# Low-rank first products of the time mixing: four float32 products against twelve products of rounded and low parts

## The chip, the cores and the metric

The kernel runs on one core of one Trainium2 chip. Its engines are TensorE (PE, with its weight loads shown apart as PEld), VectorE (DVE), ScalarE (ACT), GpSimd (POOL) and SyncE (SP), which here only issues DMA transfers. The metric is device time in microseconds (us) of one execution; less is better. A product of 128 x 128 weights with 128 x N operands is one matmul that reads both operands from SBUF and adds into PSUM.

## The reference, cut to what matters

The program is a two-layer trunk over 256 tokens of 2048 channels. Layer 0 is an RWKV-7 time mixing and a squared-ReLU MLP; layer 1 is a band attention and an MLP. The change lies in the first stage of layer 0 alone:

```python
h = modulate(rms_norm(x, g_mix[0]), sh1, sc1)
xx = token_shift(h) - h
xr, xw, xk, xv, xa, xg = [h + xx * mu[j] for j in range(6)]
v = xv @ w_v                                   # 2048 x 2048
w_log = -softplus(-(w0 + tanh(xw @ w1) @ w2)) - 0.5   # w1: 2048 x 96
a = sigmoid(a0 + (xa @ a1) @ a2)                      # a1: 2048 x 96
g = sigmoid(xg @ g1) @ g2                             # g1: 2048 x 256
```

The products concerned are `xw @ w1`, `xa @ a1` and `xg @ g1`, the "low-rank first products". All of it is float32, and the output is compared with float32 results.

## The kernel before

Activations lie with channels on the 128 partitions and the 256 tokens along the free axis, so each tensor of 2048 channels is 16 tiles of 128 x 256 (KT = 16). Large products are not computed in float32 directly. Each operand is split in two parts of type float32r: the rounded part H (a ScalarE cast, L384 for weights, L577 for activations) and the low part L, operand minus H (a VectorE subtraction, L387 for weights, L578 for activations). Three products are then summed in PSUM: H by H, H by L and L by H. The low-rank first products are the exception: they are float32 matmuls on the unsplit operands (L803, L807).

The first stage, `layer_a` up to L825, runs one loop over the 16 channel tiles n:

- SyncE loads `lw` (L787: 448 columns, the rows n of w1, a1 and g1 side by side) and the first 1024 columns of row n of w_v (`raw`, L374).
- Steps of a generator, `ada_blocks`, compute shift and scale (the adaLN of c) that later tiles need. Each step uses one 512 KB tile `rawa`: one half of them goes through TensorE (L696), the other through a VectorE multiply with accumulation (L702). A block of steps serves two tiles n (the last two blocks serve one each), eight `rawa` tiles to a block of two. At its end come L707, L712, L717 to L721.
- VectorE and ScalarE make h of tile n (L794, L796), GpSimd the difference xx (`diff`, L740), VectorE the mixed inputs (`mixed`, L745), in the order 3 (for v), 1, 4, 5 (low-rank), 2 (for k), each in one of four `mix` buffers. L820 makes the sixth in place.
- The mixed input 3 is split. Then come the four float32 products into the two accumulators `pl` (L803: w1 and a1, 96 columns each; L807: two halves of g1), and 24 matmuls of eight output tiles for the first half of v (L811 to L813).
- From n = 4 on, `v_part` adds 24 more matmuls (L773 to L775) for the second half of v, whose weights come in pieces (`v_part_weight`); n = 14 and 15 run two of them, and two more follow the loop.

After the loop the sums in `pl` go through tanh, copy and sigmoid (L830 to L832) with changes of ScalarE's function table; then the pairs of heads follow, whose projections for k and r (L418, L419) keep TensorE full for the rest of layer 0.

The order on each engine's queue is not simply the program's. The framework plans the program with its own estimate of each instruction's duration, and lets an instruction of lower rank go ahead where its operands are ready earlier in that plan; the engines then work through their queues in that fixed order. SyncE's queue is one of them, so a load that waits for its buffer holds all later loads. Buffers rotate: `raw` has six, `rawa` six, `lw` three, the weights' H and L three each.

Of the kernel before, what the change touches and what calls it, by code (L numbers as in the profile page):

```python
# [12 lines left out]
F32 = mybir.dt.float32  # L13
F32R = mybir.dt.float32r
AF = mybir.ActivationFunctionType
ALU = mybir.AluOpType
AX = mybir.AxisListType

P = 128
D = 2048  # L20
T = 256
# [9 lines left out]
HK = 8  # L31
# [304 lines left out]
class Body:  # L336
# [303 lines left out]
    def layer_a(self, st, sp):  # L640
        nc, tc, d = self.nc, self.tc, self.d
# [5 lines left out]
        with ExitStack() as s1:  # L647
# [3 lines left out]
            ph = s2.enter_context(tc.tile_pool(name="ph", bufs=1))  # L651
            s3 = s2.enter_context(ExitStack())
            pb = self.np = s3.enter_context(tc.tile_pool(name="pb", bufs=1))
            h = ph.tile([P, KT, T + 1], F32, name="h")
            first = CST_AT["ui"][0]
            nc.scalar.dma_start(out=self.csts[:, :first], in_=d["cst"][:, :first])
            for q in range(4):
# [7 lines left out]
            nc.vector.memset(h[:, :, 0:1], 0.0)  # L665
            gain = self.gp.tile([P, KT], F32, name="gain_g_mix0")
            sums = pb.tile([P, 2, KT], F32, name="sums01")
            rawa = lambda: pb.tile([P, HK * P], F32, tag="rawa", bufs=6, name="rawa")

            crow, diag = self.wp.tile([P, HK * P], F32, tag="acc", bufs=1, name="crow"), rawa()  # L670
            nc.vector.tensor_tensor(out=diag.rearrange("p (k n) -> p k n", n=P),
                                    in0=self.cst("ident").unsqueeze(1).to_broadcast([P, HK, P]),
                                    in1=self.ct[:, HK:].unsqueeze(2).to_broadcast([P, HK, P]), op=ALU.mult)
            for i in range(0, HK * P, 512):
                ps = pp.tile([P, 512], F32, tag="t", bufs=1, name="t")
# [51 lines left out]
            adab = ada_blocks()  # L727
            ss = pp.tile([P, 2, T], F32, tag="v3", bufs=1, name="v3")[:, 0, :]
            for n in range(KT):
                sq = pb.tile([P, T], F32, tag="sq", bufs=3, name="sq")  # L730
                nc.scalar.activation(sq, h[:, n, 1:T + 1], AF.Square)
                nc.tensor.matmul(ss, self.cst("ones"), sq, start=(n == 0), stop=(n == KT - 1))
            r = self.rstd(ss)
# [4 lines left out]
            def diff(n):  # L738
                xx = ph.tile([P, T], F32, tag="xx", bufs=2, name="xx")
                nc.gpsimd.tensor_tensor(out=xx, in0=h[:, n, 0:T], in1=h[:, n, 1:T + 1], op=ALU.subtract)  # L740
                return xx

            def mixed(m, n, xx):
                t = ph.tile([P, T], F32, tag="mix", bufs=4, name="mix")
                nc.vector.scalar_tensor_tensor(out=t, in0=xx, scalar=self.vec(f"mu{m}", n),  # L745
                                               in1=h[:, n, 1:T + 1], op0=ALU.mult, op1=ALU.add)
                return t
# [3 lines left out]
            pl = [pp.tile([P, 2, T], F32, tag=f"l{i}", bufs=1, name=f"l{i}") for i in range(2)]  # L751
# [6 lines left out]
            def v_part_weight():  # L758
                src = next(coming, None)
                return None if src is None else self.halves(self.raw(src))  # L760

            def v_part():

                lo, nk, i = next(parts)
                H, L = self.v_next
                nt = 8 // nk
                sums = [pp.tile([P, 2, T], F32, tag=t, bufs=1, name="t") for t in "tm"[:nt // 2]]
                for k in range(nt):
                    for kt in range(nk):
                        j, ps = nt * kt + k, sums[k // 2][:, k % 2, :]  # L770
                        a, b = (xv[:, lo + kt, i_, 0:T] for i_ in range(2))
                        last = k % 2 == 1 and kt == nk - 1
                        nc.tensor.matmul(ps, H[:, j, :], a, start=(k % 2 == 0 and kt == 0), stop=False)  # L773
                        nc.tensor.matmul(ps, H[:, j, :], b, start=False, stop=False)
                        nc.tensor.matmul(ps, L[:, j, :], a, start=False, stop=last)  # L775
                self.v_next = v_part_weight()
                for k, ps in enumerate(sums):
                    o = 8 + nt * i + 2 * k
                    o = v[:, o:o + 2, :]
                    if lo == 0:  # L780
                        nc.scalar.copy(o, ps)
                    else:
                        nc.vector.tensor_tensor(out=o, in0=o, in1=ps, op=ALU.add)

            for n in range(KT):
                lw = pb.tile([P, 448], F32, tag="lw1", bufs=3, name="lw1")
                nc.sync.dma_start(out=lw, in_=d["lora1"][n // 4, :, n % 4, :])  # L787
                raw = self.raw(d["w_v_rows"][n])
                ahead = 5 if n + 2 < KT and ends[n + 1] == n + 2 else 0
                while adab_at < min(4 * KT, 4 * ends[min(n + 1, KT - 1)] + ahead):  # L790
                    next(adab)
                    adab_at += 1
                hn = h[:, n, 1:T + 1]
                nc.vector.scalar_tensor_tensor(out=hn, in0=hn, scalar=gain[:, n:n + 1], in1=r,  # L794
                                               op0=ALU.mult, op1=ALU.mult)
                nc.scalar.activation(hn, hn, AF.Identity, bias=self.mods[(0, 0)][:, n:n + 1])  # L796
                xx = diff(n)
                first, last = n == 0, n == KT - 1
                self.split(xv, n, mixed(3, n, xx))
                H, L = self.halves(raw)  # L800

                for i, m in enumerate((1, 4)):
                    nc.tensor.matmul(pl[0][:96, i, :], lw[:, i * 96:(i + 1) * 96], mixed(m, n, xx),  # L803
                                     start=first and i == 0, stop=last and i == 1)
                t = mixed(5, n, xx)
                for i in range(2):
                    nc.tensor.matmul(pl[1][:, i, :], lw[:, 192 + i * P:192 + (i + 1) * P], t,  # L807
                                     start=first and i == 0, stop=last and i == 1)
                for i in range(8):
                    ps = pv[i // 2][:, i % 2, :]  # L810
                    nc.tensor.matmul(ps, H[:, i, :], xv[:, n, 0, 0:T], start=first and i % 2 == 0, stop=False)  # L811
                    nc.tensor.matmul(ps, H[:, i, :], xv[:, n, 1, 0:T], start=False, stop=False)
                    nc.tensor.matmul(ps, L[:, i, :], xv[:, n, 0, 0:T], start=False, stop=last and i % 2 == 1)  # L813
                if n == 3:
                    self.v_next = v_part_weight()
                for _ in range((n >= 4) + (n >= KT - 2)):
                    v_part()
                self.split(xk, n, mixed(2, n, xx))

                nc.vector.scalar_tensor_tensor(out=hn, in0=xx, scalar=self.vec("mu0", n), in1=hn,  # L820
                                               op0=ALU.mult, op1=ALU.add)
# [17 lines left out]
        with ExitStack() as s1:  # L839
# [57 lines left out]
            for slot in range(S * NPAIR + Pair.STEPS):  # L897
# [9 lines left out]
                last = self.last_pe()  # L907
                for _, _, pr in sorted(live, key=lambda x: x[:2]):
                    with tc.issue_after(last):
                        next(pr.gen)  # L910
                    last = self.last_pe()
# [329 lines left out]
```

## Time and profile before

| | us |
|---|---|
| median of 3 runs | 2670.8 |
| lowest and highest | 2667.13, 2671.81 |
| the profiled execution | 2666.43 |
| its span, first to last instruction | 2664.6 |
| the first stage, from the start to the last low-rank product | about 184 |

The stage of the change is about 7% of the span; beyond it nothing is edited. Times in the views are us from the start of the span. A group's row gives a line, an engine, an operation, the tile written and the tiles read, the shape, the count, the busy time and the mean duration in ns, and the idle time of that engine just before with what ended it. [...]

### The profile page before, as it was taken

Reading aid. Unit: us, or ns where it says so; the run is one execution under the profiler, and the core shown is the slowest. Engines: PE = TensorE matmul, PEld = TensorE weight load, DVE = VectorE, ACT = ScalarE, POOL = GpSimd, SP = SyncE. Lnnn points to the kernel's source line nnn. Section 1 sums busy time; section 2 is a strip of 40 time slices with the busy share of each in tenths; the row PEclk is TensorE's granted clock in tenths of the full one; section 3 lists DMA queues with packets and bytes.
Section 4 is the critical chain, followed back from the end, with each engine's and each line's share of the span. In section 5 each row is a group of like instructions: output and inputs, shape, how many; then the busy total and the mean of one; then the engine's idle time right before and its main releaser. Section 6 shows DMA issues by size and latency. Waiting matters only on the chain.

```text
span 2664.6 us, 58295 instructions
## 1 busy us (share of the span) xinstructions
PE 2584.6 (97%) x23596; PEld 2225.7 (84%) x23596; DVE 2107.8 (79%) x3102; ACT 1368.2 (51%) x2516; POOL 217.8 (8%) x336
## 2 busy tenths in 40 slices
PE   7998999999999999999999999999999999999997
PEld 4787778777899888888888998877898888888886
DVE  6888988888889888888888898899887556555555
ACT  3345656556455355355365554565564464453554
POOL 0001323222100000000001100000100000000002
PEclk9999999999999999999999999999999999999998
DMA  9976656566778899889998779888766555555553
GB/s 348 319 244 193 205 188 200 180 207 192 260 235 307 310 325 326 322 322 333 323 327 290 232 245 329 314 272 264 263 218 233 187 187 189 190 189 186 187 189 119
DMA packets 207149, 662.62 MB, mean 249 GB/s; under 512 B 21408, under 2 KB 54560, under 8 KB 206880
## 3 DMA queue, kind: packets, MB, share of 16 engines
q1 hardware_dynamic: 204816, 656.36, 72.9%
q8 instruction: 185, 3.03, 0.5%
q10 hardware_dynamic: 2064, 2.54, 0.3%
q14 instruction: 84, 0.69, 0.1%
HBM read 656.72 MB, written 2.10 MB: 247 GB/s over the span
## 4 chain that ended last, share of the span: by engine, by line
PE 85%; DVE 5%; issue 4%; ACT 3%; DMA 3%; POOL 1%; SPq 0%; DVEq 0%; ACTq 0%; POOLq 0%
PE pj L418 45%; PE pj L419 22%; PE pj L408 2%; PE pj L407 2%; PE pj L409 2%; DVE wL L387 2%; DMA raw<-w_ada 1%; PE iv L111 1%; ACT wH L384 1%; DVE acc L460 1%; PE gr L105 1%; PE o L407 1%; PE ms L330 1%; DMA raw<-w_q 1%; PE m L696 0%
## 5 line engine op out<-in xcount | busy, mean ns | idle before, releaser
L387 DVE TENSOR_TENSOR wL<-raw,wH 128x1024 fp32r<-128x1024 f32 x772 | 942.0, 1221 | 351.9 <-ACT wH L384 347.1
L384 ACT CAST wH<-raw 128x1024 fp32r<-128x1024 f32 x772 | 805.8, 1045 | 784.3 <-PE pj L418 625.5
L418 PE MATMUL pj<-aHL,wH 128*128 128x512 f32 x3328 | 1196.4, 401 | 1.1 <-DVE x L954 1.1
L419 PE MATMUL pj<-aHL,wL 128*128 128x256 f32 x3328 | 937.2, 282 | 0.4 <-DVE wL L387 0.3
L418 PEld LDWEIGHTS pj<-aHL,wH 128*128 128x128 f32 x3328 | 630.0, 189 | 151.7 <-issue 8.1
L418 PE MATMUL pj<-hHL,wH 128*128 128x512 f32 x2048 | 722.4, 398 | 0.0
L419 PEld LDWEIGHTS pj<-aHL,wL 128*128 128x128 f32 x3328 | 630.0, 189 | 2.5 <-issue 0.8
L419 PE MATMUL pj<-hHL,wL 128*128 128x256 f32 x2048 | 573.7, 280 | 0.9 <-DVE wL L387 0.9
L418 PEld LDWEIGHTS pj<-hHL,wH 128*128 128x128 f32 x2048 | 384.6, 188 | 94.5 <-DVE hHL L1000 0.2
L419 PEld LDWEIGHTS pj<-hHL,wL 128*128 128x128 f32 x2048 | 386.5, 189 | 1.3 <-DVE wL L387 1.2
L460 DVE SCALAR_TENSOR_TENSOR acc<-rada,ct,acc 128x1024 f32<-128x1024 f32 x256 | 327.6, 1280 | 9.6 <-DMA rada<-w_ada 9.1
L524 POOL TENSOR_TENSOR ss<-ss,sq 128x256 f32<-128x256 f32 x56 | 54.6, 975 | 1588.5 <-ACT sq L523 1588.2
L1025 DVE SCALAR_TENSOR_TENSOR x<-pj,mod,x 128x256 f32<-128x256 f32 x256 | 123.4, 482 | 58.3 <-PE pj L419 54.6
L460 DVE SCALAR_TENSOR_TENSOR acc<-raw,ct,acc 128x1024 f32<-128x1024 f32 x104 | 137.6, 1323 | 10.7 <-DMA raw<-w_ada 10.3
L997 ACT ACTIVATE t<-t 128x256 f32<-128x256 f32 x112 | 46.8, 418 | 123.7 <-DVE t L969 123.7
L407 PE MATMUL pj<-aHL,wH 128*128 128x258 f32 x384 | 109.0, 284 | 0.0
L408 PE MATMUL pj<-aHL,wH 128*128 128x258 f32 x384 | 108.9, 284 | 0.0
L409 PE MATMUL pj<-aHL,wL 128*128 128x258 f32 x384 | 108.0, 281 | 0.0
L409 PEld LDWEIGHTS pj<-aHL,wL 128*128 128x128 f32 x384 | 73.2, 191 | 0.2
L408 PEld LDWEIGHTS pj<-aHL,wH 128*128 128x128 f32 x384 | 72.6, 189 | 0.1
L407 PEld LDWEIGHTS pj<-aHL,wH 128*128 128x128 f32 x384 | 72.2, 188 | 0.2
L999 ACT ACTIVATE t<-t 128x256 f32<-128x256 f32 x128 | 53.4, 417 | 3.4
(252 smaller groups left out, 2842.8 us busy)
## 6 DMA issues: line engine op xcount, KB each, us to landing
raw<-w_up SPq DMA_DIRECT2D x256, 512.0 KB, 4.5
raw<-w_down SPq DMA_DIRECT2D x256, 512.0 KB, 4.5
rada<-w_ada SPq DMA_DIRECT2D x209, 512.0 KB, 5.6
raw<-w_ada SPq DMA_DIRECT2D x111, 512.0 KB, 4.5
rada<-w_ada_kv SPq DMA_DIRECT2D x64, 512.0 KB, 6.5
rawa<-w_ada SPq DMA_DIRECT2D x32, 512.0 KB, 6.9
rawa<-w_ada_t SPq DMA_DIRECT2D x32, 512.0 KB, 7.1
raw<-w_k SPq DMA_DIRECT2D x32, 512.0 KB, 4.2
```

The source lines that it names most:

```text
L384: nc.scalar.copy(Hf, raw)
L387: eng.tensor_tensor(out=Lf, in0=raw, in1=Hf, op=ALU.subtract)
L407: nc.tensor.matmul(ps, H[:, i, :], a(kt)[:, 0, :], start=(first and kt == 0), stop=False)
L408: nc.tensor.matmul(ps, H[:, i, :], a(kt)[:, 1, :], start=False, stop=False)
L409: ins = nc.tensor.matmul(ps, L[:, i, :], a(kt)[:, 0, :], start=False, stop=(last and kt == KT - 1))
L418: nc.tensor.matmul(ps, H[:, i, :], a(kt), start=(kt == 0), stop=False)
L419: ins = nc.tensor.matmul(ps[:, 0, :], L[:, i, :], a(kt)[:, 0, :], start=False, stop=(kt == KT - 1))
L460: nc.vector.scalar_tensor_tensor(out=self.acc, in0=raw, scalar=ck, in1=self.acc, op0=ALU.mult, op1=ALU.add)
L524: (eng or nc.gpsimd).tensor_tensor(out=self.ss, in0=self.ss, in1=sq, op=ALU.add)
L997: nc.scalar.activation(t, t, AF.Relu)
L999: nc.scalar.activation(t, t, AF.Square)
L1025: nc.vector.scalar_tensor_tensor(out=x, in0=ps[:, i, :], scalar=self.mods[(layer, 5)][:, n:n + 1], in1=x, op0=ALU.mult, op1=ALU.add)
```

## The change

The three mixed inputs 1, 4, 5 and the tile `lw` are split as the large products' operands are: ScalarE casts the rounded parts (one cast of 448 columns, three of 256), and GpSimd, not VectorE, subtracts to make the low parts. Each of the four float32 products becomes three float32r products, H by H, H by L and L by H. These twelve matmuls are placed after the v matmuls and the `v_part` of the same n, where the four were ahead of them. A new tile `lwh` has one buffer, `mh` has three. To make room, `rawa` goes from six buffers to five, `sq` (used ahead of the loop) from three to two, and `lw` from three to two.

```diff
-            rawa = lambda: pb.tile([P, HK * P], F32, tag="rawa", bufs=6, name="rawa")
+            rawa = lambda: pb.tile([P, HK * P], F32, tag="rawa", bufs=5, name="rawa")
...
-                sq = pb.tile([P, T], F32, tag="sq", bufs=3, name="sq")
+                sq = pb.tile([P, T], F32, tag="sq", bufs=2, name="sq")
...
-                lw = pb.tile([P, 448], F32, tag="lw1", bufs=3, name="lw1")
+                lw = pb.tile([P, 448], F32, tag="lw1", bufs=2, name="lw1")
...
-                for i, m in enumerate((1, 4)):
-                    nc.tensor.matmul(pl[0][:96, i, :], lw[:, i * 96:(i + 1) * 96], mixed(m, n, xx),
-                                     start=first and i == 0, stop=last and i == 1)
-                t = mixed(5, n, xx)
-                for i in range(2):
-                    nc.tensor.matmul(pl[1][:, i, :], lw[:, 192 + i * P:192 + (i + 1) * P], t,
-                                     start=first and i == 0, stop=last and i == 1)
+                lwh = pb.tile([P, 2, 448], F32R, tag="lwh", bufs=1, name="lwh")
+                nc.scalar.copy(lwh[:, 0, :], lw)
+                mhs = []
+                for m in (1, 4, 5):
+                    t = mixed(m, n, xx)
+                    mh = ph.tile([P, 2, T], F32R, tag="mh", bufs=3, name="mh")
+                    nc.scalar.copy(mh[:, 0, :], t)
+                    nc.gpsimd.tensor_tensor(out=mh[:, 1, :], in0=t, in1=mh[:, 0, :], op=ALU.subtract)
+                    mhs.append(mh)
+                nc.gpsimd.tensor_tensor(out=lwh[:, 1, :], in0=lw, in1=lwh[:, 0, :], op=ALU.subtract)
                 for i in range(8):
...
                 for _ in range((n >= 4) + (n >= KT - 2)):
                     v_part()
+                for i in range(4):
+                    mh, lo = mhs[min(i, 2)], (0, 96, 192, 192 + P)[i]
+                    w = 96 if i < 2 else P
+                    ps = pl[i // 2][:w, i % 2, :]
+                    for a, b, s_ in ((0, 0, first and i % 2 == 0), (0, 1, False), (1, 0, False)):
+                        nc.tensor.matmul(ps, lwh[:, a, lo:lo + w], mh[:, b, :], start=s_,
+                                         stop=last and i % 2 == 1 and a == 1)
                 self.split(xk, n, mixed(2, n, xx))
```

## The prediction, made before the changed kernel ran

> **What bounds the kernel now.** I read the page's first part, the busy times stretch by stretch, and then the chain of waits through the first stage.
>
> ```profile
> PE 2584.6 (97%) x23596; PEld 2225.7 (84%) x23596; DVE 2107.8 (79%) x3102; ACT 1368.2 (51%) x2516; POOL 217.8 (8%) x336
> ```
>
> Over the whole span TensorE is full, but the edit touches about 156 us only, so that share decides nothing. The next rows are busy time, with instructions in brackets, for PE, PEld, DVE, ACT and POOL, then TensorE's granted clock, the DMA share and GB/s.
>
> ```profile
> 30.00:60.00 30.00, 26.57 (x199) 20.22 (x200) 26.22 (x55) 7.57 (x14) 2.97 (x3) 0.84 1.04 375
> 90.00:120.00 30.00, 27.61 (x241) 22.24 (x241) 25.05 (x52) 10.65 (x18) 1.18 (x2) 1.00 0.89 300
> 150.00:180.00 30.00, 28.11 (x269) 24.59 (x270) 27.82 (x58) 11.36 (x20) 3.62 (x3) 1.00 0.76 260
> ...
> 30.00:186.00 156.00, 140.57 (x1260) 113.66 (x1261) 132.02 (x260) 54.96 (x89) 13.01 (x15) 0.97 0.91 313
> ```
>
> From 30 to 186 us VectorE is busy for 132.02 of 156 us (85%), TensorE for 140.57, the DMA engines for 91%; ScalarE has 101 us free and GpSimd 143. Three resources are nearly full, and the chain tells which ends last:
>
> ```profile
> 110.13 1.10 PE l L803 x4
> ...
> 118.79 0.14 PE t L775
> ...
> 119.97 1.15 DVE wL L387
> ...
> 121.16 0.38 PE t L775
> ...
> 128.11 0.13 PE t L775
> ...
> 128.87 1.23 DVE wL L387
> ...
> 130.14 0.39 PE t L775
> ...
> 131.25 0.86 PE l L803 x4
> 132.11 0.57 PE m L696 x8
> ...
> 133.71 0.86 PE l L807 x4
> ...
> 136.18 0.12 PE v L812
> ...
> 137.38 0.12 PE t L773
> ...
> 203.03 0.29 PE pj L418
> ```
>
> Between the first rows matmul follows matmul. TensorE stops at 118.93 until 121.16 and at 128.24 until 130.14, about 4 us in a block of 21.1 us (from L803 at 110.13 to L803 at 131.25), and both times what comes last is a weight's low part on VectorE. So the stage's time is TensorE's work plus VectorE's lateness; a microsecond off TensorE's queue counts if VectorE keeps up, and a microsecond onto VectorE's dense stretches counts nearly whole.
>
> **The change part by part.**
>
> *TensorE.* Four L803 records take 0.86 us, and so do four of L807. Each float32 product makes two records, as these counts for 32 products per line show:
>
> ```profile
> L803 PE MATMUL l<-mix,lw 128*96 128x256 f32 x64 | 17.9, 401 | 5.2 <-DVE mix L745 5.2
> L807 PE MATMUL l<-mix,lw 128*128 128x256 f32 x64 | 18.2, 410 | 0.0
> ...
> L577 ACT CAST aHL<-mix 128x256 fp32r<-128x256 f32 x32 | 13.0, 406 | 58.5 <-DVE mix L745 58.5
> ...
> L384 ACT CAST wH<-raw 128x1024 fp32r<-128x1024 f32 x29 | 30.0, 1043 | 3.6 <-issue 2.5 <-PE v L812 0.8 <-PE t L774 0.3
> ...
> L745 DVE SCALAR_TENSOR_TENSOR mix<-xx,vecs,h 128x256 f32<-128x256 f32 x80 | 36.3, 498 | 6.0 <-POOL xx L740 5.9
> ```
>
> One float32 product is therefore 0.43 us. Ten float32r starts lie between 136.18 and 137.38, so one costs 0.12 and three cost 0.36. 64 products (16 tiles by 4) save 0.07 us each: **-4.5 us**. Weight loads ran beside these matmuls at that pace. The 5.2 us that TensorE waits at L803 for mixed inputs I count as nothing: v's first matmul comes next, needs mixed input 3 and a cast of 0.41 us, and inherits the wait. If the wait went altogether it would be -5.2; if each of eight blocks waited for the cast as well, +3.3.
>
> *ScalarE.* Per tile three more casts of 256 (0.406 us) and one of 448, between the rows for 256 and 1024: 0.406 + 192/768 x 0.637 = 0.57. That is 1.78 us, 28.5 us in 16 tiles, hidden by 101 us of idle ScalarE: **0**. If the cover fails because a weight's cast stands behind one of these, the price is one cast a tile, 16 x 0.41 = 6.5 us.
>
> *GpSimd and VectorE.* Here is the main cost. GpSimd's subtractions have these nearest rows (min/median/max in ns), and the others show the two engines meeting:
>
> ```profile
> L740 POOL TENSOR_TENSOR xx<-h x16: 608/614/2052, 28.9 to 175.5; 128x256 f32<-128x256 f32 x16
> ...
> L231 POOL TENSOR_TENSOR al<-da,csts x16: 1082/1102/2195, 238.5 to 655.6; 128x512 f32<-128x512 f32 x16
> ...
> L125 DVE TENSOR_TENSOR sq<-s,sq x48: 375/425/1076, 218.1 to 704.0; 128x256 fp32r<-128x256 f32 x48
> ...
> 228.20 1.63 DVE L460 SCALAR_TENSOR_TENSOR acc<-raw,ct,acc 128x1024 f32<-128x1024 f32 x1
> 229.76 0.83 DVE L125 TENSOR_TENSOR sq<-s,sq 128x256 fp32r<-128x256 f32 x1
> 230.51 1.27 DVE L460 SCALAR_TENSOR_TENSOR acc<-raw,ct,acc 128x1024 f32<-128x1024 f32 x1
> ...
> 228.04 0.72 POOL L214 TENSOR_TENSOR s<-bh,pc 128x256 f32<-128x256 f32 x1 [6.03 <-DVE bh L177]
> 228.72 1.59 POOL L214 TENSOR_TENSOR s<-kh,pc 128x256 f32<-128x256 f32 x1
> ...
> L745 DVE SCALAR_TENSOR_TENSOR mix<-xx,vecs,h x80: 470/477/826, 30.5 to 179.5; 128x256 f32<-128x256 f32 x80
> ```
>
> A GpSimd subtraction of 256 takes 0.614, one of 448 by interpolation to the 512 row 0.98. 48 x 0.614 + 16 x 0.98 = 45.2 us on an engine with 143 us free, so GpSimd's own time is no bound. But at 228 us the engines hold each other up: with GpSimd's first L214 running, L460 took 1.63 where its neighbour took 1.27 (0.36 lost); GpSimd's second waited behind it (1.59 in all), and L125 behind that took 0.83 for a median of 0.425 (0.41 lost). VectorE thus loses about 0.63 of a GpSimd subtraction that it meets: 0.63 x 45.2 = 28.5 us, times its busy share of 0.85, 24 us. It has 24 us idle, a part of them in the chain from L712 to the next mixed input, where GpSimd can work too. I let half be absorbed: **+12 us**. The ends: 0, all absorbed, and 38, where each subtraction costs its whole length and nothing is absorbed (45.2 x 0.85). I take the middle because stalls of VectorE already show on the chain.
>
> [...]
>
> *Waits that are new.* The twelve matmuls need the low parts, made after the casts. Ahead of them on TensorE stand 48 matmuls of v and `v_part`, 48 x 0.12 = 5.8 us of cover (half for n below 4, where no `v_part` runs). The subtractions of a tile take 3 x 0.614 + 0.98 = 2.8 us, and 2.8 + 4 x 1.27 = 7.9 if each waits for one long VectorE instruction: mostly covered, **0**; without the cover it is the rival "late low parts". Behind a matmul waiting there stand v's matmuls of the next tile; ScalarE's next `lwh` cast (one buffer) waits for these twelve, with weight casts queued behind it; a `mix` buffer comes free only after GpSimd has read it, and VectorE's next mixed input waits for that.
>
> *Buffers.* SyncE already waits for `rawa` to come free:
>
> ```profile
> SPq L692 <- PE m L696: 37.5, 15, 5.5
> ...
> 132.74 0.38 SPq L692 DMA_DIRECT2D rawa<-w_ada  x1
> ...
> 133.46 1.22 DVE L702 SCALAR_TENSOR_TENSOR rawa<-rawa,crow 128x1024 f32<-128x1024 f32 x1
> ...
> 145.91 0.33 PE m L696
> ...
> DMA to landing us min/median/max: 4.0/6.9/9.6
> ```
>
> The tile loaded at 132.74, as the matmuls of 132.11 freed its buffer, is read at 145.91, 13.2 us later. With five buffers it waits for the next tile to be freed, by the L702 that ends at 134.68, 2.0 us later; 11 us are left, and landing takes 9.6 at most. **0**; if bursts expose it, up to 2 us in each of eight blocks, 16, and the loads of `w_v` queued behind on SyncE come late too. `lw` with two buffers is loaded with a lead of the same kind, and if it fails it holds the same queue, within the same price. `sq` is used ahead of the loop: 0, at most one cast of 0.41 for each of 16.
>
> *The end of the stage.* The last sums in `pl` come behind two `v_part` of n = 15 now:
>
> ```profile
> 185.79 0.38 ACT L830 ACTIVATE tw<-l 96x256 f32<-96x256 f32 x1
> ...
> 180.00:205.00 25.00, 22.50 (x161) 21.43 (x160) 16.41 (x20) 14.99 (x22) 0.00 (x0) 0.93 0.51 164
> ```
>
> Tanh can start up to 48 x 0.12 = 5.8 us later, and weight casts follow on ScalarE. TensorE has other matmuls for most of it (busy 22.50 of 25). Between 0 and 5.8 I take the lower part: **+1.5 us**.
>
> *Sum:* -4.5 + 12 + 1.5 = **+9.0 us**. Against the profiled execution (span 2664.6, time 2666.43) that is 2675.4; the median of the runs shown lies 4.4 higher, so against it I predict **2679.8**.
>
> **The rivals.**
>
> *Absorbed* (faster, 0.18): subtractions fit into VectorE's 24 us of idle time and the wait at L803 goes: -4.5 - 5.2 = -9.7, 2661. For it: GpSimd is free and the new matmuls have 5.8 us of slack. Against: VectorE is busy for 25.05 of 30 us between 90 and 120, and it is VectorE that TensorE waits for. It decides if under 4.5 us of VectorE's losses reach the chain.
>
> *Even* (0.22): the 80 mixed inputs have a mean of 498 for a median of 477, 1.7 us in all beside 16 subtractions of xx, so one of these costs 0.1 us now. At that price 64 make 6.4, half of it absorbed: -4.5 + 3.2 + 1.5 = 0.2, 2671. The DMA share of 0.91 also speaks for a stage that moves little either way.
>
> *Whole length* (0.17): each subtraction met costs VectorE its full time, 38 us, half absorbed: -4.5 + 19 + 1.5 = +16, 2687. It needs VectorE to issue mostly behind GpSimd; L745's maximum of 826 hints at it, the 0.36 and 0.41 above speak against.
>
> *Late low parts* (0.13): from one tile's twelve matmuls to the next run two casts (0.57 + 0.41), the 7.9 us of hindered subtractions and 12 x 0.12 of matmuls, 10.3 us; within a block the tiles now follow in about 8.6 (131.25 to L803's next group, in the row below). 1.7 us in each of eight blocks makes +13.6, on top of the forecast +22.6, 2693. It decides once GpSimd waits for a long VectorE instruction nearly every time.
>
> ```profile
> 139.78 0.59 PE L803 MATMUL l<-mix,lw 128*96 128x256 f32 x2
> ```
>
> **How the numbers follow.** The forecast has 0.30, the likeliest single case, with 2675 to 2685 as its own range. A measurement tells about 0.2%, 5.3 us, from no change. Faster: 0.18. Within: 0.22, the even case. Slower: 0.30 + 0.17 + 0.13 = 0.60. The range for 8 in 10 reaches from the absorbed case to the late low parts, 2660 to 2695, with the outer halves of these two left out.
>
> **What would show it.** Twelve float32r starts 0.12 apart per tile in place of eight records of 0.215; GpSimd at about 58 us busy or more in the stage with means well above 0.61 and 0.98; VectorE's L387, L702 and L745 with higher means than before, and longer waits of TensorE for wL. The first projection (L418), at 203.03 on the chain before, should start about 9 us later. I am wrong if VectorE's means stay as they are, or if TensorE stands at the new matmuls, or SyncE at `rawa`, for more than it did.

## The result: slower by 1.7%, and where the time lies in the profile after

| | before | after |
|---|---|---|
| median, 5 runs each | 2671.14 us | 2716.87 us |
| ratio, with its 95% interval | | 1.0174 (1.0158 to 1.0189) |
| in us (ratio x 2671) | | +46.5 (42 to 50) |
| profiled execution; its span | 2666.43; 2664.6 | 2716.87; 2714.7 |

2679.8 was predicted, 9 above the median of before, with 2695 as the upper end. The direction is right, and the size is not: the loss is five times as large. The page of the kernel after, first part, and then the first projection L418, which waits for the whole stage:

```profile
PE 2607.2 (96%) x23660; PEld 2244.2 (83%) x23660; DVE 2144.1 (79%) x3102; ACT 1394.0 (51%) x2580; POOL 295.2 (11%) x400
```

```profile
L418 PE MATMUL pj<-aHL,wH x3328: 387/396/767, 245.3 to 2608.8; 128*128 128x512 f32 x196
```

The same line of the kernel before:

```profile
L418 PE MATMUL pj<-aHL,wH x3328: 387/396/793, 202.9 to 2558.2; 128*128 128x512 f32 x196
```

The first L418 starts at 245.3 in place of 202.9, 42.4 us later; I had forecast about 9. From the first L418 to the last it is 2363.5 us after and 2355.3 before, and in the profiles of the runs below this stretch lies between 2355 and 2362, in no order that follows the edits. So the loss is made in the first stage (the two profiled spans are 50.1 us apart, and the 8 us more lie in this stretch, which varies by as much), and the start of L418 is the short measure of each experiment.

The next rows are windows of the kernel after, in the columns of those in the prediction (busy time of PE, PEld, DVE, ACT, POOL; granted clock; DMA share; GB/s):

```profile
30.00:60.00 30.00, 20.82 (x156) 15.26 (x157) 25.84 (x44) 11.23 (x25) 15.84 (x15) 0.73 0.82 284
90.00:120.00 30.00, 21.26 (x185) 17.96 (x185) 24.59 (x38) 12.85 (x25) 12.46 (x13) 0.87 0.75 259
150.00:180.00 30.00, 25.48 (x202) 21.26 (x202) 25.09 (x39) 10.26 (x19) 10.86 (x10) 0.84 0.74 240
```

Between 90 and 120 us VectorE is as busy as before (24.59 for 25.05) but gets 38 instructions done instead of 52; TensorE's busy time falls from 27.61 to 21.26 and the DMA share from 0.89 to 0.75. The granted clock, 1.00 before, is 0.87. Nothing has become full: all engines wait for one another more.

The groups of the kernel before on VectorE that answer to this (the row of L745 stands in the prediction):

```profile
L387 DVE TENSOR_TENSOR wL<-raw,wH 128x1024 fp32r<-128x1024 f32 x29 | 35.1, 1218 | 3.7 <-ACT wH L384 3.7
L702 DVE SCALAR_TENSOR_TENSOR rawa<-rawa,crow 128x1024 f32<-128x1024 f32 x29 | 34.9, 1218 | 0.7 <-DMA rawa<-w_ada_t 0.7
L578 DVE TENSOR_TENSOR aHL<-mix,aHL 128x256 fp32r<-128x256 f32 x32 | 13.3, 419 | 0.0
```

These three are counted from 25 to 186 us. And of the kernel after, from 25 to 235 us:

```profile
L745 DVE SCALAR_TENSOR_TENSOR mix<-xx,vecs,h 128x256 f32<-128x256 f32 x80 | 49.0, 658 | 4.3 <-POOL xx L740 4.3
L387 DVE TENSOR_TENSOR wL<-raw,wH 128x1024 fp32r<-128x1024 f32 x31 | 41.9, 1352 | 4.5 <-ACT wH L384 4.4
L702 DVE SCALAR_TENSOR_TENSOR rawa<-rawa,crow 128x1024 f32<-128x1024 f32 x29 | 37.9, 1320 | 0.0
L578 DVE TENSOR_TENSOR aHL<-mix,aHL 128x256 fp32r<-128x256 f32 x32 | 21.8, 684 | 3.6 <-ACT aHL L577 3.6
L809 POOL TENSOR_TENSOR mh<-mix,mh 128x256 fp32r<-128x256 f32 x48 | 55.7, 1173 | 38.1 <-ACT mh L808 38.0
L811 POOL TENSOR_TENSOR lwh<-lw,lwh 128x448 fp32r<-128x448 f32 x15 | 20.9, 1395 | 15.7 <-ACT lwh L803 14.6 <-DVE wL L387 1.1
```

Read the means. The unchanged VectorE instructions are longer: L745 80 x (658 - 498) ns = 12.8 us, L578 32 x 265 = 8.5, L387 31 x 134 = 4.2, L702 29 x 102 = 3.0, in all 28 us. GpSimd's subtractions, priced at 0.614 and 0.98 in the prediction, take 1.17 and 1.40. Both engines pay.

What TensorE waits for (us in total, times, longest), from 25 to 232 us of the kernel after:

```profile
PE t L773 <- ACT wH L384: 9.8, 4, 3.6
PE v L814 <- ACT aHL L577: 8.5, 6, 4.2
PE l L826 <- POOL lwh L811: 5.1, 7, 1.8
PE l L826 <- POOL mh L809: 3.1, 4, 1.1
```

The largest two are waits for ScalarE, an engine that is idle for more than half of the stage (busy for 53.76 of the 140 us from 60 to 200). One place shows how that comes about, in the timeline of the kernel after (start, us, instruction; in square brackets the engine's idle time before it and what ended it), GpSimd, VectorE, ScalarE and TensorE in turn:

```profile
115.73 2.06 POOL L809 TENSOR_TENSOR mh<-mix,mh 128x256 fp32r<-128x256 f32 x2 [3.53 <-ACT mh L808]
```

```profile
115.14 1.21 DVE L702 SCALAR_TENSOR_TENSOR rawa<-rawa,crow 128x1024 f32<-128x1024 f32 x1
...
116.28 0.93 DVE L578 TENSOR_TENSOR aHL<-mix,aHL 128x256 fp32r<-128x256 f32 x1
117.13 1.34 DVE L745 SCALAR_TENSOR_TENSOR mix<-xx,vecs,h 128x256 f32<-128x256 f32 x2
```

```profile
118.18 0.41 ACT L808 CAST mh<-mix 128x256 fp32r<-128x256 f32 x1 [2.23 <-DVE mix L745]
118.50 0.40 ACT L577 CAST aHL<-mix 128x256 fp32r<-128x256 f32 x1
118.81 1.04 ACT L384 CAST wH<-raw 128x1024 fp32r<-128x1024 f32 x1
```

```profile
113.75 0.28 PE L773 MATMUL t<-aHL,wH 128*128 128x256 f32 x1
113.87 0.28 PE L774 MATMUL t<-aHL,wH 128*128 128x256 f32 x1
...
119.91 0.58 PE L773 MATMUL t<-aHL,wH 128*128 128x256 f32 x1 [3.65 <-ACT wH L384]
...
123.12 0.41 PE L773 MATMUL t<-aHL,wH 128*128 128x256 f32 x1
...
125.04 0.41 PE L815 MATMUL v<-aHL,wH 128*128 128x256 f32 x1
```

While GpSimd makes two subtractions, 115.73 to 117.79, VectorE is held up by about 0.5 us (0.93 where L578 has a mean of 419 ns in the kernel before), and its mixed input is late by that and by the L702 of 1.21 us ahead of it in VectorE's own queue. ScalarE's next instruction in its queue is the cast of that input, and it stands for 2.23 us; by these rows what GpSimd costs VectorE here explains the smaller part of this wait. Behind it stands the cast of a weight (118.81), whose load was issued at 101.83 at the latest and took 7.2 us at most to land, and TensorE stands 3.65 us for that weight. VectorE, ScalarE and TensorE wait in a row, each in its own order.

Then TensorE runs slowly: nine steps lie between 123.12 and 125.04, 0.213 us each, where two matmuls at 113.75 and 113.87 are 0.12 apart (their records, 0.28 us each, overlap; what counts is the distance between starts). The granted clock, the first of the last three numbers, falls from 1.00 to 0.50:

```profile
112.00:116.00 4.00, 4.00 (x41) 3.09 (x39) 4.00 (x8) 1.55 (x5) 0.47 (x2) 1.00 0.33 72
122.00:125.80 3.80, 3.64 (x17) 3.65 (x18) 3.64 (x6) 0.00 (x0) 0.10 (x1) 0.50 0.56 196
```

Taken by single microseconds, the granted clock of this trace is 1.00 up to 119 us, 0.56 from 119 to 120, 0.50 from 120 to 125, 0.53 from 125 to 126 and 1.00 from 126 on: it fell in the last microsecond of the stop of 3.65 us and was back 6 us after TensorE went on at 119.91. In the kernel before, where the stops on the chain quoted in the prediction were 2.2 and 1.9 us, the clock stayed at 1.00 around them (118 to 132 us). What length of stop lowers the clock, and what brings it back, no run shows.

### The profile page after: what moved, and what is told of

It reads as the page before. It is cut to its first block, busy times and chain, and to the rows that moved or that the text cites. A ratio compares the mean times of both kernels' runs of the same rounds, so it can differ in the third digit from the quotient of the medians.

```text
span 2714.7 us, 58565 instructions
## 1 busy us (share of the span) xinstructions
PE 2607.2 (96%) x23660; PEld 2244.2 (83%) x23660; DVE 2144.1 (79%) x3102; ACT 1394.0 (51%) x2580; POOL 295.2 (11%) x400
## 5 line engine op out<-in xcount | busy, mean ns | idle before, releaser
L387 DVE TENSOR_TENSOR wL<-raw,wH 128x1024 fp32r<-128x1024 f32 x772 | 946.6, 1227 | 349.0 <-ACT wH L384 344.8
L384 ACT CAST wH<-raw 128x1024 fp32r<-128x1024 f32 x772 | 806.1, 1044 | 785.1 <-PE pj L418 628.4
L418 PE MATMUL pj<-aHL,wH 128*128 128x512 f32 x3328 | 1198.4, 402 | 3.2 <-ACT aHL L577 2.1
L418 PEld LDWEIGHTS pj<-aHL,wH 128*128 128x128 f32 x3328 | 631.3, 190 | 154.5 <-issue 8.1
L418 PE MATMUL pj<-hHL,wH 128*128 128x512 f32 x2048 | 722.4, 398 | 0.0
L418 PEld LDWEIGHTS pj<-hHL,wH 128*128 128x128 f32 x2048 | 384.6, 188 | 94.4 <-DVE hHL L1010 0.2
L460 DVE SCALAR_TENSOR_TENSOR acc<-rada,ct,acc 128x1024 f32<-128x1024 f32 x256 | 327.7, 1280 | 12.2 <-DMA rada<-w_ada 11.2
L1007 ACT ACTIVATE t<-t 128x256 f32<-128x256 f32 x112 | 46.8, 418 | 123.1 <-DVE t L979 123.1
L809 POOL TENSOR_TENSOR mh<-mix,mh 128x256 fp32r<-128x256 f32 x48 | 55.7, 1173 | 38.1 <-ACT mh L808 38.0
```

The source lines that it names most:

```text
L384: nc.scalar.copy(Hf, raw)
L387: eng.tensor_tensor(out=Lf, in0=raw, in1=Hf, op=ALU.subtract)
L418: nc.tensor.matmul(ps, H[:, i, :], a(kt), start=(kt == 0), stop=False)
L460: nc.vector.scalar_tensor_tensor(out=self.acc, in0=raw, scalar=ck, in1=self.acc, op0=ALU.mult, op1=ALU.add)
L809: nc.gpsimd.tensor_tensor(out=mh[:, 1, :], in0=t, in1=mh[:, 0, :], op=ALU.subtract)
L1007: nc.scalar.activation(t, t, AF.Relu)
```

## The experiments

Three theories stood beside each other at first. *Port* (a name only; no run shows what the two engines share): GpSimd's subtractions hold VectorE up, whoever reads what they make. *Queue*: the new place of the products and the waits for their casts and low parts stall TensorE. *Buffers*: with fewer of them the loads come late. Every ratio is against runs of the kernel before on the same chip, with a 95% interval; us are the ratio times 2670.

**Buffers alone.** The kernel before, with the three smaller pools of buffers:

```diff
-tag="rawa", bufs=6 ... tag="sq", bufs=3 ... tag="lw1", bufs=3
+tag="rawa", bufs=5 ... tag="sq", bufs=2 ... tag="lw1", bufs=2
```

> The kernel before with the three smaller buffer counts alone (rawa 5, sq 2, lw 2); nothing else differs. Three theories of the 46 us. Port: GpSimd's subtractions hold VectorE up, VectorE's mixed inputs come late, and TensorE stands and loses its clock. Queue: the new place of the low-rank products and the wait for their low parts stall TensorE. Buffers: the loads come late. Port and queue expect no change here, within 5 us of the 2671; buffers expects +20 us or more, and longer waits for DMA at L696 and L702.

Measured: 2670.2, ratio 1.0006 (0.9995 to 1.0017); first L418 at 204.7. The buffers cost nothing that can be told, and the prediction's 0 for them holds.

**Place alone.** The four float32 products as they are, behind v and `v_part`; no casts, no subtractions:

```diff
+mts = [mixed(m, n, xx) for m in (1, 4, 5)]          # where the four products were
...
+for i in range(4):                                  # behind v_part
+    lo = (0, 96, 192, 192 + P)[i]
+    w = 96 if i < 2 else P
+    nc.tensor.matmul(pl[i // 2][:w, i % 2, :], lw[:, lo:lo + w], mts[min(i, 2)], ...)
-tag="mix", bufs=4
+tag="mix", bufs=7                                   # and rawa with 5
```

> The kernel before with its four float32 products moved to the place that the twelve have now, behind v and v_part of the same tile; seven mix buffers hold their operands, rawa has five. No casts, no GpSimd subtractions. Port expects at most +5 us. Queue, as far as it is the place, expects +15 us or more. Buffers expects what e1_bufs gives.

Measured: 2666.25, ratio 0.9989 (0.9978 to 1.0001); first L418 at 199.6. The new place, with seven `mix` buffers for four, is no loss, and if anything a gain of 3 us. The prediction's +1.5 for the end of the stage doesn't show: tanh does start later, at 192.7 for 185.8, and L418 still comes 3.3 us earlier.

**Low parts on VectorE.** The kernel after, with both subtractions moved from GpSimd:

```diff
-nc.gpsimd.tensor_tensor(out=mh[:, 1, :], ...); nc.gpsimd.tensor_tensor(out=lwh[:, 1, :], ...)
+nc.vector.tensor_tensor(out=mh[:, 1, :], ...); nc.vector.tensor_tensor(out=lwh[:, 1, :], ...)
```

> The changed kernel with its low parts made by VectorE instead of GpSimd. VectorE then has 48 x 0.42 + 16 x 0.62 = 30 us more work of its own, about the 32 us by which its instructions got longer in the changed kernel. Port, read as load on VectorE, expects about the changed kernel's time, 2700 to 2720; if a blocked VectorE is worse than a busy one (stalls at unplanned places), 2680 to 2700. Queue expects the waits for low parts to go and 2670 to 2685.

Measured: 2681.45, ratio 1.0048 (1.0029 to 1.0068), +12.8 us; first L418 at 210.0. Groups and windows of this kernel:

```profile
L745 DVE SCALAR_TENSOR_TENSOR mix<-xx,vecs,h 128x256 f32<-128x256 f32 x80 | 35.6, 482 | 9.3 <-POOL xx L740 9.3
```

```profile
60.00:200.00 140.00, 123.96 (x1181) 106.59 (x1182) 129.67 (x267) 70.48 (x132) 13.10 (x12) 0.96 0.81 283
```

With the subtractions off GpSimd, L745 is back at 482 ns, the clock is 0.96, and 34 of the 46.5 us are gone, though VectorE now has 64 more instructions of its own. So GpSimd as the maker is the larger part of the loss, by itself or together with what waits for it. 12.8 us remain that are not GpSimd's. (The profiled execution was the fastest of four, 2670.89, so its rows show less than these 12.8 us.)

**Rounded parts alone.** The kernel after without any low part; of the three products only H by H is left, so the output lacks the low parts' share:

```diff
-for a, b, s_ in ((0, 0, first and i % 2 == 0), (0, 1, False), (1, 0, False)):
+for a, b, s_ in ((0, 0, first and i % 2 == 0),):
```

> The changed kernel without low parts: the casts stay, the GpSimd subtractions and the eight products with a low part of each tile are left out, so the low-rank products are those of the rounded operands alone. TensorE has 64 x (0.43 - 0.12) = 20 us less than the kernel before. Port expects 2650 to 2670 and a clock of 0.97 or more in the stage; queue, as far as it is the casts and the place, expects 2690 or more.

Measured: 2671.49, ratio 1.0003 (0.9992 to 1.0013); first L418 at 209.0. TensorE has 64 x (0.43 - 0.12) = 20 us less to do than in the kernel before, and none of it is in the time. That is more than *port* forecast and less than *queue* did. What it waits for:

```profile
PE t L773 <- ACT wH L384: 12.3, 6, 3.2
PE v L812 <- ACT aHL L577: 5.8, 4, 3.1
```

The same two rows with the place alone, where no cast was added (its `mix` has seven buffers, here four):

```profile
PE t L773 <- ACT wH L384: 1.2, 3, 0.5
PE v L805 <- ACT aHL L577: 3.5, 3, 2.5
```

So with the new casts on ScalarE's queue, and no GpSimd subtraction in the program, TensorE already waits some 13 us more for the casts of v's operands, in all nearly as much as in the kernel after (9.8 and 8.5). Not all of it need be the casts': with 20 us less to do TensorE reaches these places sooner. With the low parts on VectorE, where TensorE has its twelve matmuls a tile, the two rows are 2.1 and 12.1. The run can't part two readings of the time: either the casts took what TensorE gained, or TensorE's work was worth little here.

**The port alone.** The kernel before, its float32 products in the old place, with 64 GpSimd subtractions of the same sizes that nobody reads (`mix` has six buffers, the three smaller pools are as in the kernel after); beside it the same instructions on VectorE:

```diff
+for t in ms:
+    scr = ph.tile([P, T], F32R, tag="scr", bufs=2, name="scr")
+    nc.gpsimd.tensor_tensor(out=scr, in0=t, in1=t, op=ALU.subtract)      # e6: nc.vector
+scl = pb.tile([P, 448], F32R, tag="scl", bufs=1, name="scl")
+nc.gpsimd.tensor_tensor(out=scl, in0=lw, in1=lw, op=ALU.subtract)        # e6: nc.vector
```

> The kernel before (its four float32 products where they were, six mix buffers, the smaller other buffers), plus 64 GpSimd subtractions of the same shapes that read the mixed inputs and lw and write scratch that nothing reads. No casts, nothing waits for a low part. Port expects most of the loss: 2690 to 2715, L387, L702, L745 and L578 longer as in the changed kernel (means 1352, 1320, 658, 684 ns), and a lower clock. Queue, in which late low parts and casts are the cause, expects at most +8 us: under 2678.

> As e5_port, but the 64 unread subtractions run on VectorE itself: 30 us of planned work there in place of some 32 us of blocking. If VectorE's lost time alone counts, it comes out like e5_port. If blocking at places the order of the queues did not plan for is worse than planned work, it comes out like e3_dve, 2672 to 2685, with instruction means as before.

Measured on GpSimd: 2684.74, ratio 1.0066 (1.0051 to 1.0081), +17.6 us; first L418 at 220.4. On VectorE: 2673.63, ratio 1.0018 (1.0005 to 1.0031), +4.8 us; first L418 at 208.9. Groups of the first, with the unread subtractions on GpSimd:

```profile
L387 DVE TENSOR_TENSOR wL<-raw,wH 128x1024 fp32r<-128x1024 f32 x33 | 44.5, 1357 | 5.9 <-ACT wH L384 5.7
L745 DVE SCALAR_TENSOR_TENSOR mix<-xx,vecs,h 128x256 f32<-128x256 f32 x80 | 42.9, 581 | 6.2 <-POOL xx L740 6.2
L702 DVE SCALAR_TENSOR_TENSOR rawa<-rawa,crow 128x1024 f32<-128x1024 f32 x29 | 40.4, 1405 | 0.0
L578 DVE TENSOR_TENSOR aHL<-mix,aHL 128x256 fp32r<-128x256 f32 x32 | 19.7, 618 | 0.0
```

The time lies below what *port* forecast and above what *queue* did. VectorE loses 33 x 139 + 80 x 83 + 29 x 187 + 32 x 199 ns = 23 us, and 17.6 us of that, three quarters, arrive in the time, though nothing reads the subtractions (L418 is 17.5 us later in this execution). Part of them arrives where the prediction looked for it, in TensorE's waits for the low parts of weights that VectorE makes. The kernel before, then this one:

```profile
PE t L775 <- DVE wL L387: 5.8, 8, 1.6
PE t L775 <- DVE wL L387: 11.2, 9, 2.6
```

The same 64 subtractions as VectorE's own work are 27 us of busy time (17.8 and 9.2 in its groups) and cost 4.8. Why VectorE absorbs planned work better than being held up is open; the queues of the second kernel were ordered with that work in them, those of the first weren't ordered for the losses, which fits but was not tested.

**GpSimd busy without reading.** The same kernel with two fills of a constant in place of each subtraction:

```diff
-nc.gpsimd.tensor_tensor(out=scr, in0=t, in1=t, op=ALU.subtract)
+nc.gpsimd.memset(scr, 0.0)      # six a tile, and two of scl
```

> e5_port with two GpSimd memsets in place of each unread subtraction, about as long together (0.28 us for 128x256 at L850), behind each xx on GpSimd's queue. They write SBUF and read none. If VectorE and GpSimd block each other over what both read, the loss goes: 2665 to 2674, with L387, L702 and L745 near 1218, 1218 and 498 ns. If any GpSimd work in the stage blocks VectorE, it comes near e5_port, 2680 to 2690.

Measured: 2668.52, ratio 0.9993 (0.9982 to 1.0003); first L418 at 201.2.

```profile
L745 DVE SCALAR_TENSOR_TENSOR mix<-xx,vecs,h 128x256 f32<-128x256 f32 x80 | 36.0, 494 | 6.3 <-POOL xx L740 6.3
L807 POOL MEMSET scr<- 128x256 f32 x96 | 25.1, 308 | 0.0
L810 POOL MEMSET scl<- 128x448 f32 x32 | 15.0, 469 | 0.6
```

GpSimd is busy for 40 us with writing alone, and VectorE's means are those of the kernel before (L745 494 for 498 ns, L387 1219 for 1218, L702 1216 for 1218, L578 431 for 419). So it is not GpSimd's being busy or writing, as these fills do it, that holds VectorE up. The two kernels differ in that GpSimd's added instructions read SBUF in one only, and also in that the fills are shorter and stand right behind xx in GpSimd's queue; no run parts these. That it is the reading was not shown.

**A smaller dose.** The kernel after with only the 16 subtractions of `lw` on GpSimd, the 48 of mixed inputs on VectorE:

```diff
-nc.gpsimd.tensor_tensor(out=mh[:, 1, :], in0=t, in1=mh[:, 0, :], op=ALU.subtract)
+nc.vector.tensor_tensor(out=mh[:, 1, :], in0=t, in1=mh[:, 0, :], op=ALU.subtract)
```

> The changed kernel with the 48 low parts of the mixed inputs made by VectorE and only the 16 of lw by GpSimd, 15.7 us of its 45.2 us of subtractions. Port expects a loss between e3_dve's (about +12) and the changed kernel's (+46), near their share: 12 + 34 x 0.35 = +24 us, 2688 to 2700. Queue, with lw's low part last in the tile, expects the greater part of the loss to stay, 2700 or more.

Measured: 2694.18, ratio 1.0096 (1.0081 to 1.0111), +25.6 us; first L418 at 227.1. That is 12.8 us above the kernel with none on GpSimd, for 16 x 0.98 of the 45.2 us of subtractions that the prediction counts. A third of the dose makes 38% of the 34 us between the two ends.

```profile
PE l L826 <- POOL lwh L811: 7.8, 4, 4.9
```

One of these waits is 4.9 us long: here a single low part of a weight that came late stopped TensorE.

**The casts beside the port.** The unread subtractions again, now with the real casts to `lwh` and `mh` ahead of them; the products still float32 and in the old place:

```diff
+nc.scalar.copy(lwh[:, 0, :], lw)
+for t in ms:
+    nc.scalar.copy(mh[:, 0, :], t)
+    nc.gpsimd.tensor_tensor(out=mh[:, 1, :], in0=t, in1=mh[:, 0, :], op=ALU.subtract)
+nc.gpsimd.tensor_tensor(out=lwh[:, 1, :], in0=lw, in1=lwh[:, 0, :], op=ALU.subtract)
```

> e5_port with the casts as well: ScalarE casts lw and the mixed inputs 1, 4, 5 as in the changed kernel, GpSimd subtracts from these casts, and nothing reads the parts; the low-rank products stay float32 in their old place. If port and casts together make the loss (weight casts and splits behind casts that wait for late mixed inputs on ScalarE's queue), it comes near the changed kernel, 2700 to 2715. If the rest of the loss is TensorE's and ScalarE's waiting for late low parts and their two buffers, it stays near e5_port, 2682 to 2692.

Measured: 2697.15, ratio 1.0108 (1.0088 to 1.0128), +28.8 us; first L418 at 229.0. That lies between the two forecasts. Against the port alone (1.0051 to 1.0081) it is about 11 us more; the intervals barely part, and `mix` has four buffers here and six there, so the 11 us are the casts' and the smaller pool's together. TensorE's waits name the weights' casts for little of it:

```profile
PE t L773 <- ACT wH L384: 3.8, 5, 1.1
```

**Low parts made, not read.** The kernel after, except that all twelve matmuls of a tile read the rounded parts; the low parts are made and left unread, and the sums in `pl` are H by H three times over:

```diff
-nc.tensor.matmul(ps, lwh[:, a, lo:lo + w], mh[:, b, :], start=s_, ...)
+nc.tensor.matmul(ps, lwh[:, 0, lo:lo + w], mh[:, 0, :], start=s_, ...)
```

> The changed kernel whose twelve matmuls of a tile read the rounded parts three times and no low part; the subtractions run as before and nothing reads them. So far: subtractions alone +17.6 (e5_port), with casts +28 (e9_portcast), the changed kernel +46. If TensorE's wait for low parts (8.2 us at L826 in the changed kernel) and what queues behind it is the last step, it falls to 2695 to 2702. If the place and the count of the matmuls or the buffers make it, it stays at 2710 to 2720.

Measured: 2699.01, ratio 1.0101 (1.0084 to 1.0118), +27.0 us; first L418 at 232.5. TensorE does as much as in the kernel after, GpSimd and ScalarE too. So TensorE's waiting for GpSimd's results, with what it brings on, is worth 46.5 - 27.0 = 19.5 us by the ratios, and 245.3 - 232.5 = 12.8 by the start of L418. What it waits for here:

```profile
PE v L814 <- ACT aHL L577: 8.9, 7, 4.2
PE t L773 <- ACT wH L384: 7.9, 4, 3.7
```

The two waits for ScalarE are nearly those of the kernel after (8.5 and 9.8); the rows with L811 and L809, 8.2 us there, are gone. The rest of the 19.5 is not in any one row.

**The clock.** The kernel after with small float32 matmuls into a part of `pl` that nothing reads, 3 at a time ahead of the v matmuls and of `v_part`, about 40 us of work (37.3 us busy in the rows of its trace), so that it idles less long at a stretch:

```diff
+def fill():
+    with tc.issue_after(self.last_pe()):
+        for _ in range(3):
+            nc.tensor.matmul(pl[0][96:, 0, :], cst("ident")[:, 0:32], csts[:, 0:T], start=True, stop=True, ...)
```

> The changed kernel with more work for TensorE: three float32 matmuls of 128x32 by 128x256, on constants, into 32 rows of the accumulators that nothing reads, ahead of the v matmuls and ahead of v_part of each tile, at about 0.43 us each some 40 us in all. If TensorE's lowered clock (0.81 to 0.88 from 60 to 210 us) is a large part of the loss, long idle stretches get broken, the clock rises towards 1.00 and the time falls or stays, 2695 to 2717. If the clock is only a companion of idle time, the time rises by the part of the 40 us that doesn't fall into idle time, 2720 to 2750.

Measured: 2734.1, ratio 1.0247 (1.0232 to 1.0263), +66 us; first L418 at 269.9. The windows of the kernel after, and then of this one:

```profile
60.00:200.00 140.00, 112.11 (x972) 93.29 (x971) 112.52 (x180) 53.76 (x103) 57.85 (x52) 0.86 0.74 250
```

```profile
60.00:200.00 140.00, 120.64 (x948) 89.85 (x945) 99.02 (x161) 48.25 (x92) 50.48 (x48) 0.91 0.67 230
```

The clock rose from 0.86 to 0.91, and the time rose too, by about 20 us, half of the work added. Whether the higher clock gave back the other half or the idle time took it in, this run can't tell. What share of the loss is the clock's stays open.

**A version that beats both.** The place alone, as above, with every other buffer as in the kernel before (`rawa` six, `lw` three, `sq` three; `mix` seven):

> A version that could beat both: the kernel before with its four float32 products behind v and v_part (e2_move), with all its buffer counts as before and seven mix buffers. e2_move came out 0.1% faster with an interval that reaches no change. If the place gives TensorE something, 2661 to 2667 against about 2669, with an interval clear of 1; if not, within 3 us of the kernel before.

Measured: 2662.2, ratio 0.9976 (0.9965 to 0.9986), -6.4 us. Its first projection, and its windows:

```profile
L418 PE MATMUL pj<-aHL,wH x3328: 388/396/653, 197.5 to 2554.7; 128*128 128x512 f32 x196
```

```profile
60.00:200.00 140.00, 129.15 (x1174) 107.62 (x1175) 116.52 (x218) 61.38 (x99) 10.00 (x12) 1.00 0.83 286
```

The clock is 1.00 from 60 to 200 us, and L418 starts 5.4 us earlier than in the kernel before. TensorE's waits for mixed inputs at the four products fall from 5.2 to 2.6 us, and those for `wL` from 5.8 to 3.0. Two things differ from the kernel before, the place and three more `mix` buffers. Six `mix` buffers in the old place, in the kernel of the fills, gained nothing that can be told (0.9982 to 1.0003) and left these two rows at 5.2 and 5.8, so the place is the likelier cause; seven in the old place were not run, nor were the cheaper products in it.

## Why the prediction was right in direction and wrong in size

The runs give three amounts that add up to the loss: the port alone 17.6 (e5_port), the casts with it 11 (e9_portcast less e5_port), and the reading of the low parts 19.5 (after less e12_unread): 48 for 46.5. That the sum comes so near proves little: the one step between these runs that it leaves out is e12_unread less e9_portcast, the place and the cheaper products, -1.8, and with it the sum must be 46.5. The amounts go by differences of ratios whose intervals reach 4 to 5 us to either side, and by the start of L418 the same four steps are 17.5, 8.6, 12.8 and 3.5. They are not constants either: with the low parts on VectorE, casts and new waits cost 12.8 together.

1. **TensorE, -4.5.** The twelve matmuls are 0.12 apart as forecast (x12 in 1.58 us at 114.11 of the trace after). The gain doesn't arrive: 20 us less work left the time where it was in e4_rounded, though that run has the casts too. The step "a microsecond off TensorE's queue counts if VectorE keeps up" had its condition in it, and VectorE did not keep up.
2. **GpSimd and VectorE, +12.** That VectorE's instructions get longer beside GpSimd's (L745 498 to 658 ns), and the raw price, stand: 24 us of VectorE's time were worked out, 28 were lost in the kernel after and 23 with the port alone. The 38 of the rival "whole length" no run shows. The step that failed is "I let half be absorbed": three quarters arrived. That VectorE's idle 24 us don't lie where its losses fall is the likely reason; no run shows it. The forecast sign, longer waits of TensorE for `wL`, came with the port alone (11.2 for 5.8) but not in the kernel after (3.7), where TensorE waits for ScalarE instead.
3. **ScalarE's casts, 0.** This is a failed step: "hidden by 101 us of idle ScalarE". TensorE's waits for L384 and L577 are 18.3 us in the kernel after, 18.1 in e4_rounded without any GpSimd subtraction, and 4.7 with the place alone (from 25 to 232 us). The share of idle time says nothing of what stands behind a cast in the queue. At 118 us the cast of a mixed input waits 2.23 us for VectorE, the weight's cast behind it waits with it, and TensorE waits 3.65 us for the weight. The price for failing cover, 6.5, was for the cast's own 0.41 us; it should have been the wait ahead of it, those 2.23. What the step costs in time is known only roughly: about 11 us from e9_portcast, where the products stand in the old place, `mix` has fewer buffers than in e5_port, and little of it is in these rows.
4. **New waits for the low parts, 0.** Failed too, "mostly covered". The cover of 5.8 us of matmuls is there, but subtractions of 1.17 and 1.40 us, behind casts that are themselves late, use it up. The rival "late low parts" named this with +13.6, at 0.13; I had said TensorE standing at the new matmuls would make me wrong, and it stands there (8.2 us in the rows of L826), with 13 to 20 us for the whole of it (e12_unread).
5. **The rivals as alternatives.** They are written as if one or the other would come. The port's losses, late casts and late low parts lie in one chain, VectorE to ScalarE to GpSimd to TensorE, and they came together. The range's upper end, 2695, was one of them on top of the forecast; what came with all three is 2717.
6. **The clock.** It was left out. The stall of 3.65 us was followed by 6 us at a granted clock of 0.50, and the mean is 0.86 from 60 to 200 us after, where the kernel before has 1.00 between 90 and 120 and between 150 and 180. How much of the loss that is, e7_fill didn't settle.
7. **Buffers, 0: right** for the buffers alone (e1_bufs). One sign of being wrong came: SyncE's loads into `rawa` wait 127 us in all from 25 to 232 us, for 91 in the kernel before. But TensorE waits for such a load 0.8 us in all (4.4 before) and VectorE not at all, so by these rows SyncE waits for late readers and doesn't make them late; the kernel after with six `rawa` was not run. **End of the stage, +1.5: not seen.** Tanh starts 6.9 us later in e2_move (192.7 for 185.8, where the forecast had up to 5.8), and the first projection 3.3 earlier; in e11_move6 place and `mix` buffers together gain 6.4 us. I had counted the vanished wait at L803 as nothing, since "v's first matmul comes next"; it fell by half, 5.2 to 2.6.

## What to carry to other kernels

An engine's idle share was no cover for work put on its queue (ScalarE's 101 us here): look for what will stand behind the new instruction, and for how late its operand can be, since here a cast that waited 2.23 us on ScalarE stood ahead of the weight for which TensorE stopped 3.65 us. The 64 subtractions were dearer on GpSimd, beside a VectorE that is 85% busy, than as VectorE's own work (+17.6 us against +4.8), so price such work as VectorE time and add its readers' waits. And costs that meet in one chain of engines can come together: ask for the sum of the rivals before you weigh them against each other. The cheap part of an edit, here the new place of four matmuls with three more buffers, is worth a run alone (-6.4 us).

## What the hardware showed that was not expected

- With GpSimd filling SBUF for 40 us (e13_memset) VectorE's mixed inputs kept their length (494 ns for 498) and the time was 0.9993; with GpSimd subtracting, for 46 us in 48 of the 64 instructions (e5_port), they took 581 ns and the time rose by 17.6 us:

```profile
L805 POOL TENSOR_TENSOR scr<-mix 128x256 fp32r<-128x256 f32 x48 | 46.5, 985 | 33.6 <-DVE mix L745 30.8 <-DVE sums L717 1.6 <-DVE mods L719 1.1
```

- A GpSimd subtraction of 128 x 256 took 0.985 us in that run (mean of 48) and 1.17 in the kernel after, where the 16 subtractions for xx in the kernel before have a median of 0.614.
- After one stall of 3.65 us in the kernel after, TensorE's next float32r matmuls were 0.213 us apart for 0.12, at a granted clock of 0.50 for 1.00, until about 126 us, 6 us after it went on.
